# mLSTM chunks of a hybrid decoder layer: all four heads in one step, with q and k loaded a chunk ahead

## The chip, the core and the metric

The kernel runs on one core of a Trainium2 chip. The metric is the device time of one execution in microseconds (us): the median of several runs, where lower is better. The core has five engines that run their own queues of instructions in order: TensorE (PE; its weight loads are listed as PEld), VectorE (DVE), ScalarE (ACT), GpSimd (POOL) and SyncE (SP), which in this kernel issues the DMAs. Matmul results land in PSUM, here in banks of 128x512 f32; everything else on the chip lies in SBUF.

## What is computed

One decoder layer on a 1024 x 1024 input: three token mixers in parallel on the same normalised input (stick-breaking attention, an mLSTM, cross-attention into 256 memory tokens), merged by gates, then a gated MLP with a depthwise convolution. The change concerns the mLSTM alone. It has 4 heads of width 128 and walks over the 1024 positions in 8 chunks of 128, carrying a matrix state from chunk to chunk. Per head and chunk the reference computes:

```
b = cumsum(lfc);  log_d = where(causal, b[t] - b[s] + ic[s], -inf)
s = einsum('td,sd->ts', qc, kc) * exp(log_d - m_t)
w_inter = exp(m_inter - m_t)
num = s @ vc + w_inter * (c_st @ qc)
den = sum(s) + w_inter * (n_st @ qc)
h = num / maximum(abs(den), exp(-m_t))
c_new = decay * c_st + einsum('s,sv,sk->vk', wk, vc, kc)
n_new = decay * n_st + einsum('s,sk->k', wk, kc)
...
h_ml = rmsnorm(h, ml_g_out)          # per head, over its 128 channels
y_ml = sigmoid(ml_o) * h_ml
```

## The kernel before, in words

**Staging.** All large projections are done as three f32r matmuls (`mm3`, L148 to L151: high by high, high by low, low by high) in f32 accuracy. The weight of each product is split into a high and a low part just before it is used: ACT copies the high part (L136), DVE subtracts it for the low part (L137). Pairs of projections go through `seven`, a scheme of seven products; each of its units ("dense" units) is a generator with stages of 24, 36 and 24 matmuls of 128x512. `go(n)` lets the dense list run n stages on.

**The mLSTM.** q and k after their convolution, v, the output gate o and the row factors of all chunks lie in DRAM (`qk_d`, `v_d`, `o_d`, `me_d`). `ml_chunk` (L845) does one chunk for half of the heads, `g` = 0 or 1, in four steps. The loop at L952 takes the chunks from 7 down to 0. Per chunk it runs step 1 of both halves, step 3 of the two halves of the chunk before, one dense stage, step 4 of the chunk before, step 2 of both halves, and another dense stage. In this document a *block* is what PE does between two dense stages in the middle of a chunk: the transposes of step 4 for the chunk before, and then step 2.

- Step 1: load q, k (L848), v (L852) and two sets of row factors, broadcast to 128 partitions (L855); mask the first set on POOL (L858) and take its exponentials on ACT, one per head (L864); scale q by the second set on POOL (L865); k times q on PE (L868) into a bank of the `z` ring, k transposed (L873) into the `tr` ring; DVE multiplies the scores by the exponentials (L869) and scales the transposed k (L876).
- Step 2: numerator and denominator on PE (L883, L884), a bank of `tr`; the new state (L888), a bank of `z`; DVE updates the state (L895) and works out the divisor (L902 to L905); ACT divides while it copies out (L908), squares and sums (L910, one read of the accumulator each); the gate is loaded (L912).
- Step 3: `rstd_cols` (one small DVE operation, L155, and a power on POOL, L157); DVE scales h by it (L916).
- Step 4: transposes on PE (L920) into `tr`; DVE multiplies by g_out and by the gate (L922); store (L923).

**Buffers.** Each of the PSUM rings `tr` and `z` has two banks here. q, k and v of a half share one tile of the `y` ring, which has two buffers: so the two halves of a chunk hold both, and a next chunk's load has to wait until the matmuls of step 2 (L884, L888), which read v, are done. The row factors use the `me` ring (two buffers).

**Order.** The text is written in one order for all engines; a scheduler then sets each engine's queue, so that work from the dense units lies between the steps, and puts in the waits. All DMAs of the stretch stand in SP's one queue.

Of the kernel before, what the change touches and what calls it, by code (L numbers as in the profile page):

```python
# [42 lines left out]
def tile_hybrid_layer(ctx: ExitStack, tc: tile.TileContext, xT, memT, vecs, w_t, w_n, w_kv, w_if,  # L43
# [16 lines left out]
    def nm(s):  # L60
# [4 lines left out]
            "mw": 8, "sm": 22, "px": 2}  # L65
    late = [None]

    def T(shape, tag, dt=F32, bufs=None):
        pool = {"mw": mlp, "mst": mlp, "ga": mlp, "gm": mlp,  "px": late[0]}.get(tag, sb)
        return pool.tile(shape, dt, tag=tag, name=nm(tag), bufs=bufs or BUFS[tag])  # L70
# [444 lines left out]
    def rows_tile():  # L515
        return T([R, P], "mw")

    def suffix(cur, op):
        s = 1
        while s < P:  # L520
            nxt = rows_tile()
# [9 lines left out]
    def gate_rows():  # L531
        gi, gf = rows_tile(), rows_tile()
# [3 lines left out]
        e = rows_tile()  # L536
        nc.scalar.activation(e, gf, AF.Abs)
        nc.scalar.activation(e, e, AF.Exp, scale=-1.0)
        u = rows_tile()
        nc.vector.tensor_scalar(u, e, 1.0, None, op0=ALU.add)  # L540
        lu = rows_tile()
# [5 lines left out]
        bcur = rows_tile()  # L547
        nc.vector.scalar_tensor_tensor(bcur, gf, 0.0, lu, op0=ALU.min, op1=ALU.subtract)

        bcum = suffix(bcur, ALU.add)  # L550
        ga = T([R, P], "ga", bufs=1)
        nc.vector.tensor_sub(ga, gi, bcum)
        amax = suffix(ga, ALU.max)
# [18 lines left out]
        gm = T([R, P], "gm", bufs=1)  # L572
        nc.gpsimd.tensor_scalar(gm, amax, mprev, -1.0, op0=ALU.max, op1=ALU.mult)
        ge = rows_tile()
        nc.scalar.activation(ge, gm, AF.Exp, bias=mprev)
        gw = rows_tile()
        nc.scalar.activation(gw, ga, AF.Exp, bias=gm[:, 0:1])
        gfl = rows_tile()
# [229 lines left out]
    cw = const.tile([P, 40], F32, tag="cw", name="cw")  # L808
# [26 lines left out]
    def ml_o(j):  # L835
        def done(g, c):
            nc.scalar.activation(c, c, AF.Tanh, scale=0.5)
            nc.vector.tensor_scalar(c, c, 1.0, 0.5, op0=ALU.add, op1=ALU.mult)
            nc.sync.dma_start(o_d[j + g], c)
# [3 lines left out]
    def ml_chunk(g, c, state, hm, kw):  # L843
        hd = (2 * g, 2 * g + 1)
        qv = T([P, 4 * P + 258], "y")  # L845
        qk = qv[:, :4 * P].rearrange("p (i h t) -> p i h t", i=2, h=2)
        for i in range(2):
            nc.sync.dma_start(qk[:, i], qk_d[4 * i + 2 * g:4 * i + 2 * g + 2, :, ts(c)].rearrange("h p t -> p h t"))  # L848
        q, k = qk[:, 0], qk[:, 1]
        vx = qv[:, 4 * P:].rearrange("p (h v) -> p h v", h=2)  # L850
        nc.gpsimd.memset(vx[:, :, 128:129], 1.0)
        nc.sync.dma_start(vx[:, :, :P], v_d[c, :, 256 * g:256 * g + 256].rearrange("p (h v) -> p h v", h=2))  # L852
        me = T([P, 2, 2, P], "me")
        for i in range(2):
            nc.sync.dma_start(me[:, i].rearrange("p h t -> p (h t)"),  # L855
                              me_d[i, 4 * c + 2 * g:4 * c + 2 * g + 2].rearrange("h t -> (h t)")
                              .partition_broadcast(P))
        nc.gpsimd.affine_select(out=me[:, 0], in_=me[:, 0], pattern=[[0, 2], [-1, P]], compare_op=ALU.is_ge,  # L858
                                fill=-1e30, base=0, channel_multiplier=1)
        dt_ = T([P, 2, P], "mw")  # L860
        qt = T([P, 2, P], "mw")
        for i, h in enumerate(hd):
            r = 4 * c + h
            nc.scalar.activation(dt_[:, i], me[:, 0, i], AF.Exp, bias=cols[:, 0, r:r + 1])  # L864
            nc.gpsimd.tensor_mul(qt[:, i], q[:, i], me[:, 1, i])  # L865
        pz = bank("z")
        for i in range(2):
            nc.tensor.matmul(pz[:, ts(i)], k[:, i], q[:, i], start=True, stop=True)  # L868
        nc.vector.tensor_mul(dt_.rearrange("p h t -> p (h t)"), dt_.rearrange("p h t -> p (h t)"), pz[:, :2 * P])  # L869
        if c > 0:  # L870
            pk = bank("tr")
            for i, h in enumerate(hd):
                nc.tensor.transpose(pk[:, ts(i)], k[:, i], ident)  # L873
            for i, h in enumerate(hd):
                r = 4 * c + h
                nc.vector.tensor_scalar(kw[:, i], pk[:, ts(i)], cols[:, 1, r:r + 1], None, op0=ALU.mult)  # L876
        yield
        pn = bank("tr")
# [528 lines left out]
```

## Time and profile before

| what | us |
|---|---|
| runs, median (lowest to highest of 3) | 1693.62 (1692.54 to 1694.19) |
| the profiled execution, its own time | 1690.06 |
| its span, first to last instruction | 1688.3 |
| PE busy in the span | 1654.0 (98%) |
| DVE, ACT, POOL busy in the span | 1196.5, 822.9, 72.1 |
| the mLSTM chunks, first to last PE instruction | from 533.7 to 677 in the span |

A span is the time on the profiler's clock from the first to the last instruction; the execution's own time has some 2 us more around it. A wait is an idle stretch of an engine with what ended it. In the timeline, consecutive instructions of one kind are merged into one row ("x4"), and matmuls overlap: what a matmul costs is the distance to the start of the next, not its own duration.

### The profile page before, as it was taken

The page shows a single profiled execution, that of the slowest core. Times are in us where ns is not written, and L with a number is a line of the kernel's source. Part 1 is how long each engine was busy: PE and PEld are TensorE (multiplying, and loading weights), DVE is VectorE, ACT ScalarE, POOL GpSimd, SP SyncE. Part 2 cuts the span into 40 slices and gives each one's busy share as a digit, 9 for nine tenths or more (in the row PEclk, how much of TensorE's full clock was granted, in tenths as well). Part 3 has the DMA queues.
Part 4 walks back from the last instruction along what each step waited for, and adds up shares of the span by engine and source line. Part 5 has one row for each costly group of instructions (what it writes and reads, how often), then busy time and mean ns, then how long its engine had stood idle before and what let it go on. Part 6 is the DMA issues. An engine that isn't in the chain of part 4 may idle for free.

```text
span 1688.3 us, 21433 instructions
## 1 busy us (share of the span) xinstructions
PE 1654.0 (98%) x7927; PEld 1336.0 (79%) x7927; DVE 1196.5 (71%) x1752; ACT 822.9 (49%) x1293; POOL 72.1 (4%) x149
## 2 busy tenths in 40 slices
PE   8999999999999999999999999999999999999999
PEld 4777777787777888777788887788888888788887
DVE  5648777768944665555457748998777887789864
ACT  4547677645545455555412334565545554543531
POOL 1000000020001222100000000000000000000000
PEclk9999999999999999999999999999999999999999
DMA  8421011333325656432765355232322222486042
GB/s 290 150 64 32 26 39 51 106 113 125 122 91 151 168 170 192 145 103 91 253 195 186 107 181 181 69 107 75 103 85 76 75 75 75 162 323 237 30 142 73
DMA packets 99069, 212.73 MB, mean 126 GB/s; under 512 B 13184, under 2 KB 41088, under 8 KB 98964
## 3 DMA queue, kind: packets, MB, share of 16 engines
q1 hardware_dynamic: 98964, 211.35, 37.2%
q8 instruction: 63, 1.03, 0.2%
q14 instruction: 42, 0.34, 0.1%
HBM read 156.71 MB, written 54.61 MB: 125 GB/s over the span
## 4 chain that ended last, share of the span: by engine, by line
PE 83%; DVE 5%; DMA 5%; ACT 4%; issue 1%; SPq 0%; POOL 0%; POOLq 0%; ACTq 0%; DVEq 0%
PE ps_pj L149 13%; PE ps_pj L150 13%; PE ps_pj L151 13%; PE ps_pv L150 5%; PE ps_pv L151 5%; PE ps_pv L149 5%; PE ps_tr L149 4%; PE ps_tr L151 4%; PE ps_tr L150 4%; PE ps_z L151 2%; PE ps_z L150 2%; PE ps_z L149 2%; PE ps_tr L434 1%; PE ps_pv L448 1%; DMA y<-qk_d 1%
## 5 line engine op out<-in xcount | busy, mean ns | idle before, releaser
L150 PE MATMUL ps_pj<-h,whi 128*128 128x512 f32 x620 | 243.4, 393 | 0.0
L136 ACT ACTIVATE whi<-raw 128x512 fp32r<-128x512 f32 (+1 forms) x112 | 93.6, 835 | 184.1 <-PE ps_pj L150 89.0
L149 PE MATMUL ps_pj<-h,whi 128*128 128x512 f32 x412 | 163.6, 397 | 0.5 <-DVE U L1050 0.5
L149 PE MATMUL ps_pj<-pg,whi 128*128 128x512 f32 x396 | 155.2, 392 | 0.9 <-ACT U L708 0.9
L151 PE MATMUL ps_pj<-pg,wlo 128*128 128x512 f32 x380 | 148.1, 390 | 0.2 <-DVE wlo L137 0.2
L150 PEld LDWEIGHTS ps_pj<-h,whi 128*128 128x128 f32 x620 | 116.5, 188 | 24.5 <-issue 1.0
L151 PE MATMUL ps_pj<-h,wlo 128*128 128x512 f32 x332 | 130.8, 394 | 0.5 <-DVE wlo L137 0.4
L818 DVE SCALAR_TENSOR_TENSOR y<-U,vec,y 128x1023 f32<-128x1023 f32 x88 | 112.4, 1279 | 7.7 <-ACT y L816 7.7
L422 DVE TENSOR_TENSOR_SCAN U<-U 128x512 f32<-128x512 f32 (+3 forms) x96 | 88.6, 965 | 30.6 <-ACT U L415 29.7
L149 PEld LDWEIGHTS ps_pj<-h,whi 128*128 128x128 f32 x412 | 77.4, 188 | 17.1 <-DVE U L1050 0.9
L137 DVE TENSOR_TENSOR wlo<-raw,whi 128x1024 fp32r<-128x1024 f32 x54 | 66.0, 1222 | 33.5 <-ACT whi L136 33.5
L149 PEld LDWEIGHTS ps_pj<-pg,whi 128*128 128x128 f32 x396 | 74.3, 188 | 18.1 <-ACT U L708 1.5
L151 PEld LDWEIGHTS ps_pj<-pg,wlo 128*128 128x128 f32 x380 | 71.3, 188 | 15.7 <-DVE wlo L137 0.6
L136 ACT ACTIVATE whi<-pg 128x512 fp32r<-128x512 f32 (+1 forms) x59 | 43.4, 737 | 74.6 <-PE ps_pv L150 20.1
L150 PE MATMUL ps_pj<-pg,whi 128*128 128x512 f32 x188 | 74.8, 398 | 0.0
L151 PEld LDWEIGHTS ps_pj<-h,wlo 128*128 128x128 f32 x332 | 62.3, 188 | 14.7 <-DVE wlo L137 1.4
L150 PE MATMUL ps_pv<-h,whi 128*128 128x512 f32 x164 | 63.8, 389 | 0.0
L137 DVE TENSOR_TENSOR whi<-raw,whi 128x512 fp32r<-128x512 f32 x58 | 40.4, 696 | 31.7 <-ACT whi L136 31.7
L816 ACT ACTIVATE y<-U,vec 128x1024 f32<-128x1024 f32 x44 | 54.6, 1241 | 14.5 <-DVE U L721 14.4
L151 PE MATMUL ps_pj<-h,whi 128*128 128x512 f32 x156 | 60.8, 390 | 0.0
L151 PE MATMUL ps_tr<-pg,wlo 128*128 128x512 f32 x144 | 56.1, 389 | 0.0
L137 DVE TENSOR_TENSOR wlo<-raw,wlo 128x512 fp32r<-128x512 f32 x58 | 40.3, 694 | 21.3 <-ACT wlo L136 21.0
(429 smaller groups left out, 4294.8 us busy)
## 6 DMA issues: line engine op xcount, KB each, us to landing
raw<-in_w_t_dram SPq DMA_DIRECT2D x29, 512.0 KB, 4.9
gate_d<-U SPq DMA_DIRECT2D x24, 512.0 KB, 3.4
U<-gate_d SPq DMA_DIRECT2D x24, 512.0 KB, 3.7
pg<-in_w_up_dram SPq DMA_DIRECT2D x22, 512.0 KB, 3.4
act_d<-y SPq DMA_DIRECT2D x22, 512.0 KB
pg<-in_w_t_dram SPq DMA_DIRECT2D x21, 512.0 KB, 3.3
raw<-in_w_dn_dram SPq DMA_DIRECT2D x18, 512.0 KB, 4.6
raw<-in_w_o_dram SPq DMA_DIRECT2D x16, 512.0 KB, 3.7
```

The lines of the kernel that those rows point to most:

```text
L136: nc.scalar.activation(hi, src, AF.Copy)
L137: (eng or nc.vector).tensor_sub(lo, src, hi.bitcast(F32))
L149: nc.tensor.matmul(out, lh, rh, start=start, stop=False, skip_group_check=more)
L150: nc.tensor.matmul(out, lh, rl, start=False, stop=False, skip_group_check=more)
L151: nc.tensor.matmul(out, ll, rh, start=False, stop=stop, skip_group_check=more)
L422: nc.vector.tensor_tensor_scan(f[:, a, 1:w + 1], f[:, a, 1:w + 1], f[:, a, 1:w + 1], 1.0 if o == 0 else f[:, a, 0:1], op0=ALU.mult, op1=AL ...
L434: nc.tensor.transpose(pt[:, a, ts(j)], g[:, a, ts(j)], ident)
L448: nc.tensor.matmul(pv[64 * a:64 * a + 64, ts(rb % 4)], sbv[s // 2][:, s % 2, (2 * p + a) * 64:(2 * p + a + 1) * 64], wt[:, a, ts(j)], star ...
L816: nc.scalar.activation(out, u, AF.Identity, bias=bias, scale=taps[0])
L818: nc.vector.scalar_tensor_tensor(out[:, :S - s], u[:, s:], taps[s], out[:, :S - s], op0=ALU.mult, op1=ALU.add)
```

## The change

`ml_chunk` handles all four heads of a chunk in one call. Elementwise operations on 128x128 or 128x256 become one on 128x512, with the per-head factors broadcast along the last axis. q and k of a chunk share one `y` tile, and a new function `ml_load` loads them with the row factors of the next chunk right after step 1 of the present one, and before the dense stage. v has two buffers of its own from the `hf` ring for the whole loop (`vx`), with the ones column written once. Scaling q moves from POOL to DVE. The squares are taken by one ACT operation and summed by a DVE reduction. g_out is multiplied into the gate o before that is stored (`ml_o`), so that step 4 multiplies once. A copy of the decay of each head is taken on POOL (`dec`). The buffers of the gate rows are recut so that the `mw` ring needs four buffers of 128x512 and not eight of 128x256. The matmuls are the same in number and shape.

```diff
-    def ml_chunk(g, c, state, hm, kw):
...
+    def ml_load(c):
+        qk = T([P, 2, MLH, P], "y")
         for i in range(2):
-            nc.sync.dma_start(me[:, i].rearrange("p h t -> p (h t)"),
...
+            nc.sync.dma_start(qk[:, i], qk_d[4 * i:4 * i + 4, :, ts(c)].rearrange("h p t -> p h t"))
+        rows = []
         for i in range(2):
+            rows.append(T([P, MLH, P], "me"))
+            nc.sync.dma_start(rows[i].rearrange("p h t -> p (h t)"),
+                              me_d[i, 4 * c:4 * c + 4].rearrange("h t -> (h t)").partition_broadcast(P))
+        return qk[:, 0], qk[:, 1], *rows
+
+    def ml_chunk(c, loaded, state, vx, hm, kw):
...
+        for g in range(2):
+            nc.sync.dma_start(vx[g][:, :, :P], v_d[c, :, 256 * g:256 * g + 256].rearrange("p (h v) -> p h v", h=2))
+        dt_ = T([P, MLH, P], "mw")
+        qt = T([P, MLH, P], "mw")
+        for h in heads:
+            nc.scalar.activation(dt_[:, h], mm[:, h], AF.Exp, bias=cols[:, 0, r0 + h:r0 + h + 1])
+        dec = small(MLH)
+        nc.gpsimd.tensor_copy(dec, ee[:, :, 0])
+        nc.vector.tensor_mul(qt, q, ee)
...
+        nc.vector.tensor_mul(dt_, dt_, pz)
...
+            nc.vector.tensor_mul(kw, pk, spread_cols(cols[:, 1, r0:r0 + 4]))
         yield
...
+        for g in range(2):
+            pn = bank("tr")[:, :258].rearrange("p (h v) -> p h v", h=2)
             for i in range(2):
...
+                nc.tensor.matmul(pn[:, i], dt_[:, h], vx[g][:, i], start=first, stop=True)
+            if c > 0:
+                pst = bank("z")[:, :258].rearrange("p (h v) -> p h v", h=2)
...
+        nc.scalar.activation(qt, hm, AF.Square)
+        ss = small(MLH)
+        nc.vector.tensor_reduce(ss, qt, axis=AX.X, op=ALU.add)
...
+        rr = rstd_cols(ss, MLH, MLD)
+        nc.vector.tensor_mul(hm, hm, spread_cols(rr))
         yield
...
+        nc.vector.tensor_mul(og, py, og)
...
+    loaded = ml_load(NCH - 1)
     for c in range(NCH - 1, -1, -1):
...
+        new = ml_chunk(c, loaded, state, vx, kept[:, 0], kept[:, 1])
+        next(new)
+        if old:
+            next(old)
+        if c:
+            loaded = ml_load(c - 1)
         go(1)
+        if old:
+            next(old)
+        next(new)
         go(1)
```

PE's queue at the block of chunk 6, before (ps_tr and ps_z are banks of the two rings, mst the state, mw the factors, pg h or the scaled k, y holds q, k, v):

```order
L920 MATMUL ps_tr_4651<-ident,pg_4364 128x128 x2
L920 MATMUL ps_tr_4657<-ident,pg_4364 128x128 x2
L888 MATMUL ps_z_4668<-y_4544,pg_4364 128x129 x2
L888 MATMUL ps_z_4689<-y_4570,pg_4364 128x129 x2
...
L883 MATMUL ps_tr_4663<-mst_4459,mw_4556 128x129
L884 MATMUL ps_tr_4663<-y_4544,mw_4555 128x129
```

The same block of the changed kernel (hf are the two tiles of v):

```order
L916 MATMUL ps_tr_4587<-ident,pg_4342 128x128 x4
L883 MATMUL ps_tr_4595<-mst_4430,mw_4512 128x129
L884 MATMUL ps_tr_4595<-hf_4343,mw_4511 128x129
...
L888 MATMUL ps_z_4600<-hf_4343,pg_4342 128x129 x2
L883 MATMUL ps_tr_4610<-mst_4443,mw_4512 128x129
L884 MATMUL ps_tr_4610<-hf_4344,mw_4511 128x129
```

The four transposes now fill one bank, and the second numerator (ps_tr_4610) takes that same bank again within the block, after the first numerator and the first state update.

SP's queue around the loads for chunk 5, before (y are the two tiles of q, k and v of that chunk, raw and pg are weights):

```order
L689 DMA raw_4910<-in_w_t_dram 128x1024
L692 DMA pg_5224<-in_w_t_dram 128x1024
L923 DMA y_d<-mw_4471 128x2x128
...
L848 DMA y_4741<-qk_d 128x2x128 x2
L852 DMA y_4741<-v_d 128x2x128
L855 DMA me_4746<-me_d 128x256 x2
L848 DMA y_4767<-qk_d 128x2x128 x2
```

In the changed kernel the loads of q and k for chunk 4 (y_4697) stand ahead of those of v for chunk 5 (hf):

```order
L680 DMA raw_4798<-in_w_t_dram 128x1024
L838 DMA y_4697<-qk_d 128x4x128 x2
L683 DMA pg_5049<-in_w_t_dram 128x1024
L918 DMA y_d<-mw_4453 128x4x128
L858 DMA hf_4343<-v_d 128x2x128
...
L842 DMA me_4700<-me_d 128x512
```

The q and k loads moved one chunk forward in the queue; the v loads and the row factors did not move as far.

POOL's queue, before, from chunk 5 to chunk 4 (sm in L157 is the power of step 3 of chunk 5, half by half; the mask L858 is on the row factors of chunk 4):

```order
L157 TENSOR_TENSOR sm_5007<-sm_5005,nhalf 128x2
L858 AFFINE_SELECT me_4958<-me_4958 128x256
L157 TENSOR_TENSOR sm_5013<-sm_5011,nhalf 128x2
L865 TENSOR_TENSOR mw_4965<-y_4953,me_4958 128x128 x2
L858 AFFINE_SELECT me_4984<-me_4984 128x256
```

After, from chunk 6 to chunk 4 (the powers sm_4694, sm_4869, sm_5037 are those of chunks 6, 5 and 4; the masks me_4700, me_4875, me_5043 those of chunks 4, 3 and 2):

```order
L157 TENSOR_TENSOR sm_4694<-sm_4692,nhalf 128x4
L855 AFFINE_SELECT me_4700<-me_4700 128x512
L864 COPY sm_4852<-me_4702 128x4
L855 AFFINE_SELECT me_4875<-me_4875 128x512
L157 TENSOR_TENSOR sm_4869<-sm_4867,nhalf 128x4
L864 COPY sm_5020<-me_4877 128x4
L855 AFFINE_SELECT me_5043<-me_5043 128x512
L157 TENSOR_TENSOR sm_5037<-sm_5035,nhalf 128x4
```

The products with q are gone from POOL; the mask of the chunk after next stands ahead of the power for chunks 5 and 4.

DVE's queue, before, from the scaling of h in chunk 4 (sm_5212 and sm_5218 are the two powers) to the products of its block (raw and wlo are a weight page and its low part):

```order
L916 TENSOR_SCALAR pg_4364<-pg_4364,sm_5212 128x128 x2
...
L916 TENSOR_SCALAR pg_4364<-pg_4364,sm_5218 128x128 x2
...
L715 TENSOR_TENSOR raw_5222<-raw_5222 128x512
L137 TENSOR_TENSOR wlo_5319<-raw_4910,wlo_5319 128x512
...
L137 TENSOR_TENSOR whi_5337<-pg_4912,whi_5337 128x512
L703 TENSOR_TENSOR pg_5526<-raw_5524,pg_5526 128x512
L137 TENSOR_TENSOR wlo_5419<-raw_5222,wlo_5419 128x512
L700 TENSOR_TENSOR U_5243<-U_5243,ps_pv_5227 128x512
L922 SCALAR_TENSOR_TENSOR mw_5084<-ps_tr_5265,vec,mw_5084 128x128 x2
L922 SCALAR_TENSOR_TENSOR mw_5105<-ps_tr_5271,vec,mw_5105 128x128 x2
```

After, at the same place:

```order
L912 TENSOR_TENSOR pg_4342<-pg_4342,sm_5037 128x512
L706 TENSOR_TENSOR raw_5047<-raw_5047 128x512
L137 TENSOR_TENSOR wlo_5133<-raw_4798,wlo_5133 128x512
L705 TENSOR_TENSOR U_4973<-U_4973,ps_pv_4975 128x512
L869 TENSOR_TENSOR mw_5014<-mw_5014,ps_z_5023 128x512
L874 TENSOR_TENSOR pg_4342<-ps_tr_5029,cols 128x512
L137 TENSOR_TENSOR whi_5151<-pg_4800,whi_5151 128x512
L694 TENSOR_TENSOR pg_5303<-raw_5301,pg_5303 128x512
L137 TENSOR_TENSOR wlo_5207<-raw_5047,wlo_5207 128x512
L691 TENSOR_TENSOR U_5068<-U_5068,ps_pv_5052 128x512
L917 TENSOR_TENSOR mw_4956<-ps_tr_5090,mw_4956 128x512
```

The order is the same, but for one scaling, one product of the scores, one scaled k and one product with the gate, each 512 wide, in place of two or four smaller ones. The low part that stands third here frees the weight page into which raw_5301 of the eighth row is loaded.

## Rows read from the trace of the kernel before

**Rows 1.** The page: its head and the busy times of the whole span.

```profile
span 1688.3 us, 21433 instructions
...
PE 1654.0 (98%) x7927; PEld 1336.0 (79%) x7927; DVE 1196.5 (71%) x1752; ACT 822.9 (49%) x1293; POOL 72.1 (4%) x149
```

**Rows 2.** Waits, 520 to 690 us (who <- releaser: us in total, times, longest us).

```profile
PE ps_z L868 <- DMA y<-qk_d: 5.8, 4, 2.2
PE ps_pj L149 <- ACT U L708: 1.1, 2, 0.9
...
DVE pg L916 <- POOL sm L157: 22.6, 16, 3.7
```

**Rows 3.** Timeline of PE (start us, us, operation; in brackets idle before, releaser).

```profile
588.83 0.68 PE L868 MATMUL ps_z<-y 128*128 128x128 f32 x4 [1.60 <-DMA y<-qk_d]
...
644.88 0.68 PE L868 MATMUL ps_z<-y 128*128 128x128 f32 x4 [2.20 <-DMA y<-qk_d]
```

**Rows 4.** Timeline of SP, 560 to 605 us: a load of q and k.

```profile
583.07 0.90 SPq L848 DMA_DIRECT2D y<-qk_d  x2
```

**Rows 5.** Landing times of DMAs: q and k, row factors, weights (last column, page).

```profile
DMA to landing us min/median/max: 2.4/3.2/4.6
...
DMA to landing us min/median/max: 3.9/5.6/6.2
...
raw<-in_w_t_dram SPq DMA_DIRECT2D x29, 512.0 KB, 4.9
```

**Rows 6.** Timeline of PE over one chunk: step 1, the block, the next step 1.

```profile
551.66 0.60 PE L868 MATMUL ps_z<-y 128*128 128x128 f32 x4
...
558.49 0.60 PE L920 MATMUL ps_tr<-ident,pg 128*128 128x128 f32 x4
558.92 1.06 PE L888 MATMUL ps_z<-y,pg 128*128 128x129 f32 x8
559.74 0.48 PE L149 MATMUL ps_pj<-h,wlo 128*128 128x512 f32 x1
560.05 0.45 PE L883 MATMUL ps_tr<-mst,mw 128*128 128x129 f32 x2
...
561.82 0.48 PE L150 MATMUL ps_pj<-h,wlo 128*128 128x512 f32 x1
...
567.15 0.60 PE L868 MATMUL ps_z<-y 128*128 128x128 f32 x4
```

**Rows 7.** Timeline of DVE at the same block.

```profile
558.69 0.69 DVE L700 TENSOR_TENSOR U<-U,ps_pv 128x512 f32<-128x512 f32 x1 [0.88 <-PE ps_pv L151]
559.29 1.12 DVE L922 SCALAR_TENSOR_TENSOR mw<-ps_tr,vec,mw 128x128 f32<-128x128 f32 x4
```

**Rows 8.** DVE by shape, 528 to 690 us (count | busy us, mean ns | idle before, releaser).

```profile
L916 DVE TENSOR_SCALAR pg<-pg,sm 128x128 f32<-128x128 f32 x32 | 9.7, 343 | 22.6 <-POOL sm L157 22.6
...
L714 DVE TENSOR_TENSOR U<-U,ps_pv 128x512 f32<-128x512 f32 x7 | 4.8, 684 | 7.9 <-ACT U L713 7.9
```

**Rows 9.** ACT by shape, 528 to 690 us: the squares.

```profile
L910 ACT ACTIVATE mw<-pg 128x128 f32<-128x128 f32 x32 | 9.6, 310 | 0.0
```

**Rows 10.** Timeline of ACT at the same block: the copies out of step 2.

```profile
562.57 0.63 ACT L908 ACTIVATE pg<-ps_tr,sm 128x128 f32<-128x128 f32 x2 [3.25 <-DVE sm L905]
...
563.68 0.61 ACT L908 ACTIVATE pg<-ps_tr,sm 128x128 f32<-128x128 f32 x2
```

**Rows 11.** POOL by shape, 528 to 690 us: the powers and the mask.

```profile
L157 POOL TENSOR_TENSOR sm<-sm,nhalf 128x2 f32<-128x2 f32 x16 | 11.2, 699 | 22.4 <-DVE sm L155 22.4
L858 POOL TENSOR_SCALAR_AFFINE_SELECT me<-me 128x256 f32<-128x256 f32 x14 | 6.0, 432 | 29.6 <-DMA me<-me_d 29.6
L157 POOL TENSOR_TENSOR sm<-sm,nhalf 128x8 f32<-128x8 f32 x1 | 2.0, 2011 | 2.9 <-DVE sm L155 2.9
```

**Rows 12.** Timeline of POOL: a power behind a mask that waits for its rows.

```profile
586.77 0.41 POOL L858 TENSOR_SCALAR_AFFINE_SELECT me<-me 128x256 f32<-128x256 f32 x1 [2.68 <-DMA me<-me_d]
587.14 0.70 POOL L157 TENSOR_TENSOR sm<-sm,nhalf 128x2 f32<-128x2 f32 x1
```

More of the change, by code (lines that the diff above doesn't have):

```diff
@@ new lines, in ml_load, with spread_cols @@
+        rows = []
+        for i in range(2):
+            rows.append(T([P, MLH, P], "me"))
[3 more added lines that the diff above has]
+    def ml_chunk(c, loaded, state, vx, hm, kw):
+        q, k, mm, ee = loaded
+        heads = range(MLH)
+        r0 = 4 * c
+        def spread_cols(x):
+            return x.unsqueeze(2).to_broadcast([P, MLH, P])
+        nc.gpsimd.affine_select(out=mm, in_=mm, pattern=[[0, MLH], [-1, P]], compare_op=ALU.is_ge,
+                                fill=-1e30, base=0, channel_multiplier=1)
+        for g in range(2):
[7 more added lines that the diff above has]
+        nc.vector.tensor_mul(qt, q, ee)
+        pz = bank("z").rearrange("p (h t) -> p h t", h=MLH)
+        for h in heads:
+            nc.tensor.matmul(pz[:, h], k[:, h], q[:, h], start=True, stop=True)
+        nc.vector.tensor_mul(dt_, dt_, pz)
+        if c > 0:
+            pk = bank("tr").rearrange("p (h t) -> p h t", h=MLH)
+            for h in heads:
+                nc.tensor.transpose(pk[:, h], k[:, h], ident)
+            nc.vector.tensor_mul(kw, pk, spread_cols(cols[:, 1, r0:r0 + 4]))
@@ L877, in ml_chunk @@
         yield
[L878 removed]
+        rd = small(MLH)
         first = state[0] is None
[L880 to L891 removed]
+        for g in range(2):
+            pn = bank("tr")[:, :258].rearrange("p (h v) -> p h v", h=2)
+            for i in range(2):
+                h = 2 * g + i
+                if not first:
+                    nc.tensor.matmul(pn[:, i], qt[:, h], state[g][:, i], start=True, stop=False)
+                nc.tensor.matmul(pn[:, i], dt_[:, h], vx[g][:, i], start=first, stop=True)
+            if c > 0:
+                pst = bank("z")[:, :258].rearrange("p (h v) -> p h v", h=2)
+                for i in range(2):
+                    nc.tensor.matmul(pst[:, i], kw[:, 2 * g + i], vx[g][:, i], start=True, stop=True)
@@ L904, in ml_chunk @@
[L904 to L912 removed]
+                    state[g] = T([P, 2, 129], "mst", bufs=2)
@@ new lines, in ml_chunk @@
+                    nc.vector.tensor_copy(state[g], pst)
+                else:
+                    for i in range(2):
+                        nc.vector.scalar_tensor_tensor(state[g][:, i], state[g][:, i], dec[:, 2 * g + i:2 * g + i + 1],
+                                                       pst[:, i], op0=ALU.mult, op1=ALU.add)
+            d = rd[:, 2 * g:2 * g + 2]
+            nc.vector.scalar_tensor_tensor(d, pn[:, :, 128], -1.0, cols[:, 2, r0 + 2 * g:r0 + 2 * g + 2],
+                                           op0=ALU.mult, op1=ALU.max)
@@ L923, in ml_chunk @@
-        nc.sync.dma_start(y_d[1][2 * g:2 * g + 2, :, ts(c)].rearrange("h p t -> p h t"), og)
+        py = bank("tr").rearrange("p (h t) -> p h t", h=MLH)
+        for h in heads:
+            nc.tensor.transpose(py[:, h], hm[:, h], ident)
+        nc.vector.tensor_mul(og, py, og)
+        nc.sync.dma_start(y_d[1][:, :, ts(c)].rearrange("h p t -> p h t"), og)
         yield
```

126 lines of the change are left out of this document (28 added, 98 removed).

## Prediction, made before the changed kernel ran

> **What bounds the kernel now.** First the page's head: PE is busy in 98% of the span, 1654.0 of 1688.3 us, and no other engine in more than 79% (the weight loads, which overlap PE) or 71% (DVE) [rows 1]. So a saving on DVE, ACT or POOL counts only if PE waits for that engine. Second the waits in the mLSTM's stretch, to see for what PE waits there: 5.8 us in four waits of L868, the product of k and q, for the load of q and k, and 1.1 us for the copy of a weight's high part, L708 on ACT [rows 2]. These 6.9 us are all that PE can win in this stretch, 0.4% of the kernel. The large wait of the same view is DVE's own, 22.6 us at L916 for POOL's power, in 16 times [rows 2]. PE waits there for nothing, so that wait is covered today. Third the timelines. The longest waits of L868 end at 588.83 (1.60 us) and 644.88 (2.20 us) [rows 3]. The load for the first was issued at 583.07 [rows 4]; loads of q and k take 3.2 us in the median, up to 4.6, from issue to landing [rows 5]. It was issued late since its tile also holds v, which the matmuls of the chunk before still read. The path of the end here is then: block, buffer of `y`, load, L868.
>
> **The matmuls.** They are as many and as large as before, so PE's busy time stays: 0. The rest is a question of waits.
>
> **q and k a chunk ahead.** The load for chunk c-1 stands behind step 1 of chunk c. It needs the other `y` tile, free since step 1 of chunk c+1, and its user comes a whole chunk later. Two blocks are 8.66 us (block to step 1) and 6.83 us (step 1 to block) apart in the shorter chunks, 15.5 us [rows 6], and the load needs at most 4.6 [rows 5]. A few us of queueing in SP's queue remain covered. All four waits go: -5.8 us [rows 2]. Nothing else is late at L868 itself: it needs only q, k and a `z` bank.
>
> **PE's wait for ACT.** ACT loses the accumulator reads and 32 squares of 310 ns (9.6 us in all [rows 9]) for 8 of 512 elements; it waited more than it worked at this place (3.25 us at 562.57 [rows 10]). The L708 wait stems from a weight page that lands late, and SP's queue ahead of it is recut. Bounds: 0 and -1.1 [rows 2]. I take -0.4, since the queue still holds loads ahead of it.
>
> **DVE.** L916 has 32 operations of 343 ns, 9.7 us [rows 8]; now there are 8 of 512 elements, some 0.69 each by L714 [rows 8], 5.5 us. The scores, the scaled k and the gate's product shrink likewise, while scaling q (8 x 0.69 = 5.5 us) comes from POOL, and a reduction is new. DVE is 71% busy and PE doesn't wait for it: 0 as work. Only the times at which DVE gives back a bank or a factor count; they are the next two terms.
>
> **The bank of the block (new).** All four transposes go to one `tr` bank, and the second numerator needs that bank again within the block. Call the block's start t (558.49 in rows 6). The transposes take 0.43 us (558.49 to 558.92), a numerator group 0.89 (half of 560.05 to 561.82) and half of the state updates 0.41 (half of 558.92 to 559.74) [rows 6]: PE asks at t + 1.73. DVE began the product at 559.29, t + 0.80, behind another operation [rows 7]; one of 512 elements takes 0.68 by L714 [rows 8], and so ends at t + 1.48. That is 0.25 us early: 0. One more operation of 0.6 ahead of it (558.69 to 559.29 [rows 7]) gives 0.35 in each of seven blocks, 2.5 us; a whole product in the way gives 7 x 0.7 = 4.9. A gain is excluded, as PE waits for no bank there today. I take 0, since the rows of this very block are the nearest, and keep 0 to 4.9.
>
> **POOL's queue (new).** The mask of chunk c-2 now stands ahead of the power of chunk c for c = 5, 4 and 2 (and 7, where there is slack). It waits for a load into the buffer that the exponentials of chunk c-1 still read; these lie on ACT among the copies out of the block, at 562.57 to 564.3 in the trace of before [rows 10], so I set them done at t + 4.5. The issue takes 0.45 (half of 0.90 [rows 4]), landing 5.6 (3.9 to 6.2 [rows 5]): t + 10.55. The mask has twice the 256 elements that took 432 ns, 0.86 at most; the power of four columns lies between the 699 ns of two and the 2011 of eight, by proportion 1.14 [rows 11]: t + 12.5. Such a blocking shows once in the trace of before: the mask at 586.77 had waited 2.68 us for its rows, with the power right behind it [rows 12]. What is queued behind the power's user: DVE's scaling of h (0.69, t + 13.2), then up to six operations of some 0.6, then the block's product (0.68), on which PE waits through the bank. For chunk 5, six stand between: t + 17.5; PE asks at t + 15.5 + 1.73 = t + 17.2: 0.3 us. For chunk 2, four stand between: t + 16.3, no wait. For chunk 4, a low part behind the scaling frees a weight page (t + 14.4); its load lands 4.9 later [rows 5], t + 19.3, and a sum, a low part, another sum and the product follow, 0.69 + 0.6 + 0.69 + 0.68: t + 22.0. This chunk has 12 more dense matmuls at 0.23 us (561.82 to 567.15 holds 23 [rows 6]): PE asks at t + 17.2 + 2.8 = t + 20.0, a wait of 2.0. Together +2.3 us. Lower bound 0 (the exponentials come early, the rows land in 3.9); the upper one is a rival.
>
> A wide operation makes its users wait until it is whole: the bank, today freed in quarters, comes free in one piece, which is the wait priced above at 0 by rows 6 and 7. The Trainium skill ("Perfetto Trace Analysis", section "Optimizing Scalar/DVE Operations") speaks against this change: "If Scalar/Vector aren't saturated, but are causing bubbles on other engines, breaking up instructions may allow work to be completed sooner." By that, the wide product would cost PE a bubble at each block; no row here shows such a bubble yet, and the rival that follows from it is the third below.
>
> **Sum.** -5.8 - 0.4 + 0 + 2.3 = -3.9 us. The profiled execution took 1690.06; that gives 1686.2. The median of the runs is 1693.62, 3.6 higher than the profiled execution; the same step from there gives **1689.7 us**. About 0.2% (3.4 us) is what a measurement of this kernel can tell from no change, so this is just beyond it.
>
> **The rivals.**
>
> 1. *Nothing new arises.* The bank is in time, and the rows land before the power is due. For: DVE's present 22.6 us of waiting cost PE nothing. Against: the order of POOL's queue. -5.8 - 0.9 = -6.7: 1686.9.
> 2. *q and k are loaded no earlier in effect.* Their issue stands in SP's one queue behind loads that wait for weight pages, so it comes when it came before. For: all loads of the stretch share that queue. Against: the order has the loads a chunk ahead, and 15 us of slack. 0: 1693.6.
> 3. *The bank of the block decides.* DVE has one more operation ahead of the wide product: 7 x 0.35 = 2.5. For: only 0.25 us of room. Against: rows 7 have the product in time. -3.9 + 2.5 = -1.4: 1692.2.
> 4. *Slower: POOL's queue blocks DVE in three chunks.* Where the row factors land x us after t + 10.55, the scaling, the weight page behind it and the product are x later in each. The waits become 0.3 + x, x - 0.9 and 2.0 + x. At x = 3.5 (for instance the load queued behind a weight load of 4.9 [rows 5]) they are 3.8, 2.6 and 5.5, in all 11.9; less 6.2 it is +5.7: 1699.3. It passes zero at x = 1.6 (1.9 + 0.7 + 3.6 = 6.2) and the 0.2% at x = 2.7. For: the mask waited 29.6 us for rows in this stretch already [rows 11]. Against: two loads a chunk take the place of four.
>
> **How the numbers follow.** The forecast has 0.45: its own range of 1687.4 to 1691.5 lies mostly below the 1690.2 that counts as faster, so 0.36 of it is faster and 0.09 the same. Rival 1 has 0.17, faster. Rival 2 has 0.11 and rival 3 has 0.13, the same; rival 4 has 0.14, 0.11 of it slower. Faster 0.53, same 0.36, slower 0.11. The range goes from 1685.8 (rival 1 and a little of the matmuls' own scatter) to 1695.5, which leaves out most of rival 4 and little else.
>
> **What the changed profile would show.** Right: no wait of L868 for q and k; a PE wait of about 2 us in chunk 4, at the second numerator, released by DVE; a mask on POOL that waits for its rows right ahead of a power in chunks 5 and 4; PE busy 1654 as before. Wrong: waits for the load at the product of k and q (rival 2); a wait of some 0.35 us at the second numerator in every block (rival 3); DVE waiting over 5 us at one scaling of h, and PE behind it at the block (rival 4); PE waits outside of 533 to 690 us that were not there before, which this working takes as unchanged.

## The result, and the profile after

| | kernel before | changed kernel |
|---|---|---|
| median of four runs, us | 1693.90 (1692.54 to 1695.92) | 1683.33 (1682.28 to 1685.04) |
| ratio, with its 95% interval | | 0.9938 (0.9920 to 0.9955) |
| profiled execution, us | 1690.06 | 1682.28 |
| its span, us | 1688.3 | 1680.5 |

The changed kernel is faster by 10.6 us in these runs. A second set (the experiments below) gave 1684.50 against 1692.48, ratio 0.9949 (0.9936 to 0.9962). The forecast of 1689.7, 4 us below the kernel before, had the sign right and less than half of the size, and the time lies below its range (1685.8 to 1695.5).

The head of the page of the changed kernel: PE's busy time is 1.8 us below that of [rows 1], with as many matmuls.

```profile
span 1680.5 us, 21066 instructions
...
PE 1652.2 (98%) x7927; PEld 1337.1 (80%) x7927; DVE 1193.2 (71%) x1682; ACT 819.1 (49%) x1237; POOL 51.8 (3%) x95
```

In its waits from 520 to 690 us there is no row of PE left: the 5.8 and 1.1 us of [rows 2] are gone. What remains is on the other engines (who <- releaser: us in total, times, longest us):

```profile
POOL me L855 <- DMA me<-me_d: 87.8, 6, 37.6
POOL sm L157 <- DVE sm L155: 69.6, 6, 15.2
...
DVE pg L912 <- POOL sm L157: 11.7, 8, 3.3
```

DVE still waits for the power, 11.7 us in place of 22.6, and PE still does not notice.

**How the difference adds up.** From 530 to 700 us both kernels issue the same dense matmuls in the same order, so their starts can be compared one by one, and a wait's cost read as the growth of the distance between two starts. In this stretch the changed kernel gains 9.25 us:

| where | recorded idle before | distance gained |
|---|---|---|
| the four waits of L868 | 5.76 | 6.70 |
| the two waits for L708 (548.80 and 684.62) | 1.09 | 1.63 |
| block in one piece, no dense matmul within it; 0.31 of it at 616.89, a cause that no wait shows | none | 0.80 |
| the rest | none | 0.12 |

Over the whole trace the two profiled spans differ by 7.8 us, as 1.4 us are lost ahead of 530 us. About 1 us of that is a stretch at a lower clock from 417 us on, which the second profile of the kernel before (below) has too.

The first row of the table in two timelines (start, us, operation). Before: step 1 of a chunk, with the wait of 1.60 us of [rows 3] between the second row and the third.

```profile
586.18 0.39 PE L151 MATMUL ps_pv<-h,wlo 128*128 128x512 f32 x1
586.40 0.60 PE L868 MATMUL ps_z<-y 128*128 128x128 f32 x4
...
589.49 0.48 PE L149 MATMUL ps_pj<-h,whi 128*128 128x512 f32 x1
```

After:

```profile
585.13 0.39 PE L151 MATMUL ps_pv<-h,wlo 128*128 128x512 f32 x1
585.36 1.05 PE L868 MATMUL ps_z<-y 128*128 128x128 f32 x8
586.25 0.60 PE L873 MATMUL ps_tr<-ident,y 128*128 128x128 f32 x4
586.61 0.48 PE L149 MATMUL ps_pj<-h,whi 128*128 128x512 f32 x1
```

From the last dense matmul ahead to the first behind, 3.31 us became 1.48: 1.83 (1.84 unrounded) for 1.60 of recorded idle. The wait costs 0.24 more than its idle time, in each of the four places (0.23 to 0.24). Idle time is counted from the modelled end of a matmul (0.39 us behind its start for a dense one), while the next dense matmul usually starts after 0.23 us.

### The profile page after: what moved, and what is told of

The parts are those of the page before. It is cut to its first block, busy times and chain, and to the rows that moved or that the text cites. A ratio compares the mean times of both kernels' runs of the same rounds, so it can differ in the third digit from the quotient of the medians.

```text
span 1680.5 us, 21066 instructions
## 1 busy us (share of the span) xinstructions
PE 1652.2 (98%) x7927; PEld 1337.1 (80%) x7927; DVE 1193.2 (71%) x1682; ACT 819.1 (49%) x1237; POOL 51.8 (3%) x95
## 4 chain that ended last, share of the span: by engine, by line
PE 90%; DVE 4%; ACT 4%; DMA 1%; issue 1%; SPq 0%; POOLq 0%; ACTq 0%; DVEq 0%
PE ps_pj L150 14%; PE ps_pj L149 14%; PE ps_pj L151 14%; PE ps_pv L151 6%; PE ps_pv L149 6%; PE ps_pv L150 6%; PE ps_tr L149 4%; PE ps_tr L151 4%; PE ps_tr L150 4%; PE ps_z L151 2%; PE ps_z L150 2%; PE ps_z L149 2%; PE ps_tr L434 2%; PE ps_pv L448 1%; PE ps_z L226 1%; PE ps_z L1005 1%
## 5 line engine op out<-in xcount | busy, mean ns | idle before, releaser
L436 ACT ACTIVATE y<-ps_tr 128x1024 f32<-128x1024 f32 (+3 forms) x48 | 39.1, 814 | 31.6 <-PE ps_tr L434 31.2
```

Of the source, the lines that this page charges most:

```text
L436: nc.scalar.activation(wt[:, :, :w], pt[:, :, :w], AF.Copy)
```

## The experiments

Each kernel ran on a chip with the kernel before beside it; the ratio is to that one.

**The two kernels once more.** No edit.

> The kernel before once more, unchanged, against itself. Its profiled execution took 1690.06 us, its runs 1692.5 to 1695.9. Theory V (the waits for q and k differ from execution to execution, and the profile caught a mild one): ratio 1.000, and a second profile shows more than 5.8 us of PE waiting for q and k, or waits of the same size elsewhere. Rival F (the two kernels differ elsewhere, all through the span): the second profile's waits for q and k are 5.8 us again within 0.5, and its span is longer by some other rows.

Measured: 1693.98 against 1692.48, ratio 1.0002 (0.9993 to 1.0012). The second profile has 5.1 us of waits for q and k, so theory V's larger wait did not come. Nor do the two kernels differ elsewhere, as rival F had it: the second profiles of both (a2 below is that of the changed kernel) differ by 9.2 us, and 9.7 are gained from 530 to 700 us alone. The span of a1 is 1692.9, 4.6 us longer than the first; by distances some 3.5 us of growth lie behind 700 us. Part of it is in no wait. After the wait of 2.21 us at 644.49, the dense matmuls run 0.43 us apart for eight instructions:

```profile
644.49 0.68 PE L868 MATMUL ps_z<-y 128*128 128x128 f32 x4 [2.21 <-DMA y<-qk_d]
...
645.61 0.63 PE L150 MATMUL ps_pj<-h,whi 128*128 128x512 f32 x1
646.03 0.63 PE L151 MATMUL ps_pj<-h,whi 128*128 128x512 f32 x1
```

By stretches (us, busy times by engine, then the granted clock, DMA share, GB/s), the granted clock in that place was 0.55, mostly the lower level of 1.2 GHz:

```profile
640.00:645.00 5.00, 2.79 (x18) 2.31 (x17) 1.78 (x4) 1.82 (x5) 1.97 (x4) 1.00 0.74 185
645.00:648.00 3.00, 3.00 (x11) 2.44 (x10) 2.56 (x8) 0.69 (x2) 1.28 (x3) 0.55 0.69 231
```

In the first profile the same wait (2.20 us, [rows 3]) was followed by this:

```profile
645.00:648.00 3.00, 3.00 (x17) 2.58 (x18) 1.94 (x5) 0.53 (x2) 0.72 (x2) 1.00 0.84 266
```

So a wait of the same length is paid a second time in one execution (8 x 0.20, 1.6 us) and not in another. Each of the profiles but the first shows at least one such stretch behind a wait, near 417 or near 1065 us or at both; the first profile of before has none (clock 1.000), and only three of the 72 other runs of that kernel were faster. The clock of 68 of these is on record: three have 1.000 and took 1689.78 to 1691.04 us, and the 25 with 0.997 took 1694.6 in the mean. The Trainium skill ("TensorE: Matmul & The Clock Gate", section "What's actually happening") says that the window over which activity is judged is free-running and "doesn't reset when your kernel starts". By that, one and the same wait may or may not lower the clock; the two traces agree with it.

> The changed kernel once more, for a tighter ratio and a second profile. Ratio expected 0.9938 (0.992 to 0.9955 so far), that is 1683 where the kernel before takes 1693.6; no wait of PE for q and k, and PE idle in 533 to 690 us below 0.5 us.

Measured: 1684.50, ratio 0.9949 (0.9936 to 0.9962); no wait of PE for q and k, as expected.

**One half of the change: v apart.** In the kernel before; q and k of the four heads then come in two loads and not in four:

```diff
-        qv = T([P, 4 * P + 258], "y")
+        qk = T([P, 2, MLH, P], "y")
...
+    vx = [T([P, 2, 129], "hf") for _ in range(2)]
```

> The kernel before with one part of the change: q and k of a chunk share a tile, v has two tiles of its own, so that the next chunk's q and k no longer wait for the matmuls that read v. The text order of the loads and all narrow operations stay. Theory B (the buffer is what matters): all of the gain, ratio 0.9935 to 0.996, no PE wait for q and k. Rival W (the wide operations and the emptier POOL bring part of it): some -6 us, ratio 0.9965, and waits for ACT or DVE remain in 533 to 690 us.

Measured: 1687.87, ratio 0.9973 (0.9963 to 0.9984). The waits for q and k are gone, and a new one stands there:

```profile
PE ps_tr L883 <- DVE mw L922: 3.6, 2, 2.2
```

This is the wait for DVE and POOL that the prediction feared for the changed kernel, in two of the chunks that it named (5 and 2), but in the narrow kernel. A chunk has two masks there, and in chunk 5 each stands on POOL ahead of a power (the block that uses the h of this chunk began at 592.10):

```profile
584.54 0.41 POOL L858 TENSOR_SCALAR_AFFINE_SELECT me<-me 128x256 f32<-128x256 f32 x1 [14.19 <-DMA me<-me_d]
584.92 0.70 POOL L157 TENSOR_TENSOR sm<-sm,nhalf 128x2 f32<-128x2 f32 x1
588.09 0.41 POOL L858 TENSOR_SCALAR_AFFINE_SELECT me<-me 128x256 f32<-128x256 f32 x1 [2.47 <-DMA me<-me_d]
588.46 0.71 POOL L157 TENSOR_TENSOR sm<-sm,nhalf 128x2 f32<-128x2 f32 x1
```

The rows for the second half landed 3.5 us after those of the first, the second scaling started at 589.21, and twelve DVE operations later the products of the block ran at 595.45 to 596.57, while PE had asked for the bank at 594.

**The other half: wide, but v in the tile again.** The changed kernel with

```diff
-        qk = T([P, 2, MLH, P], "y")
+        halves = [T([P, 4 * P + 258], "y") for _ in range(2)]
```

and the loads written at the chunk's start.

> The changed kernel with that one part undone: q, k and v of a half share a tile again (two buffers hold one chunk), loaded at the chunk's start; all four heads in one wide operation as in the changed kernel (only the scaling of q goes half by half). Theory B: the waits for q and k come back, 5 to 9 us, ratio 0.999 to 1.001. Rival W: the wide operations keep 2 to 4 us, ratio 0.9975 to 0.999.

Measured: 1683.21, ratio 0.9945 (0.9932 to 0.9959), and no PE wait from 520 to 690 us. Both theories fall: with the buffer shared as before, nothing is late. So the shared buffer alone does not make q and k late. SP's queue at the block of chunk 5 (which starts at 575.47 here) shows why: q and k of the second half are issued at 578.96, 3.5 us after the block's start, and the row factors stand behind them.

```profile
576.83 0.37 SPq L924 DMA_DIRECT2D y_d<-mw  x1
577.44 0.90 SPq L841 DMA_DIRECT2D y<-qk_d  x2
578.44 0.43 SPq L863 DMA_DIRECT2D y<-v_d  x1
578.96 0.93 SPq L841 DMA_DIRECT2D y<-qk_d  x2
579.98 0.42 SPq L863 DMA_DIRECT2D y<-v_d  x1
580.49 0.42 SPq L847 DMA_DIRECT2D me<-me_d  x1
```

In the kernel before, that load was issued at 583.07 [rows 4], 5.4 us after the block's start (577.70). The buffer held the first half's load back to 580.07, 2.4 us after that start (2.0 in a4); then this stood in SP's queue ahead of the second half's:

```profile
581.00 0.46 SPq L848 DMA_DIRECT2D y<-qk_d  x1
581.55 0.44 SPq L852 DMA_DIRECT2D y<-v_d  x1
582.09 0.89 SPq L855 DMA_DIRECT2D me<-me_d  x2
```

Each load holds the queue for some 0.45 us.

**Only the order of the loads.** The kernel before, with q and k of both halves first, then v, then the row factors:

```diff
+        for g in range(2):
+            for i in range(2):
+                nc.sync.dma_start(qk[:, i], ...)
+        for g, (_, vx, _) in enumerate(out):
+            nc.sync.dma_start(vx[:, :, :P], ...)
+        for g, (_, _, me) in enumerate(out):
+            for i in range(2):
+                nc.sync.dma_start(me[:, i].rearrange("p h t -> p (h t)"), ...)
```

> The kernel before with another order of the loads alone: q and k of both halves first, then v of both, then the row factors of both. The tiles, their two buffers and all operations stay. Theory Q (PE waited for the second half's q and k since they stood on SP behind v and the row factors of the first half, some 1.4 us of issues, and behind two stores): the four waits shrink from 5.1-5.8 us to below 2, and the time falls by 3 to 6 us, ratio 0.9965 to 0.998. Rival B (the buffer comes free too late, whatever the order): the waits stay above 4 us, ratio 0.999 to 1.001.

Measured: 1688.70, ratio 0.9974 (0.9964 to 0.9985). The four waits for q and k are gone with no buffer freed, which theory Q had; but the row factors, now last and still four loads, came late. The exponentials wait for them, DVE's product with the scores for the exponentials, and so PE waited for DVE instead:

```profile
PE ps_tr L892 <- DVE mw L931: 1.9, 2, 1.1
PE ps_tr L929 <- DVE pg L885: 0.9, 1, 0.9
```

By distances, 6.7 us are won at L868 and 3.4 lost at two blocks.

**Only the squares.** The kernel before with

```diff
-        for i in range(2):
-            nc.scalar.activation(qt[:, i], hm[:, i], AF.Square, accum_out=ss[:, i:i + 1])
+        nc.scalar.activation(qt, hm, AF.Square)
+        nc.vector.tensor_reduce(ss, qt, axis=AX.X, op=ALU.add)
```

> The kernel before with one part of the change: the squares of a half are taken by one ACT operation of 256 elements and summed by a DVE reduction, in place of two with a read of the accumulator each. Theory A (the PE wait of 0.9 us at 548.8 was for a copy that stood on ACT behind these squares): that wait goes or falls below 0.4 us, the four waits for q and k stay at 5 to 6 us, time -0.5 to -1.6 us, ratio 0.9985 to 1.000. Rival S (it stood there since a weight came late through SP's queue): the wait stays, 0.7 to 1.2 us, ratio 0.9995 to 1.0005.

Measured: 1695.00, ratio 1.0014 (1.0005 to 1.0023). The wait for L708 stays:

```profile
549.63 0.50 PE L149 MATMUL ps_pj<-pg,whi 128*128 128x512 f32 x1 [0.85 <-ACT U L708]
```

Theory A falls. The ratio lies above the ranges of both theories: this edit by itself costs some 2 us in the narrow kernel (PE now waits also for DVE, 1.0 us at L883). What L708 was late for is a weight page. On DVE, before and then with v apart:

```profile
540.96 0.69 DVE L702 TENSOR_TENSOR hf<-pg 128x512 f32<-128x512 f32 x1 [4.10 <-DMA pg<-in_w_t_dram]
```

```profile
539.32 0.69 DVE L702 TENSOR_TENSOR hf<-pg 128x512 f32<-128x512 f32 x1 [1.42 <-DMA pg<-in_w_t_dram]
```

The page came 1.6 us sooner there and PE's wait at 548.80 was gone: behind that page lie, in order, DVE's L721, ACT's tanh (L782), the copies out of step 2, the squares and L708. So far this is what rival S named as the cause. In the changed kernel, though, the page came no sooner (its DVE waited for it until 543.38); there DVE's product on which the tanh waits follows one operation behind the page and not four, and the copy (L699, 548.15) stands ahead of the squares. Several things shorten this chain; which of them is enough was not tried one by one.

**v apart, and wide row factors.** a3, with two loads and one mask a chunk in place of two and one for each half:

```diff
-        me = T([P, 2, 2, P], "me")
-        for i in range(2):
-            nc.sync.dma_start(me[:, i].rearrange("p h t -> p (h t)"), ...)
+        for i in range(2):
+            rows.append(T([P, MLH, P], "me"))
+            nc.sync.dma_start(rows[i].rearrange("p h t -> p (h t)"), ...)
...
```

> The kernel with v apart (a3) and one more part of the change: the row factors of all four heads in one tile for each set, two loads and one mask a chunk in place of four and two, and the copy of the decay. All else stays narrow. Theory M (the 3.6 us that PE waited there for DVE in chunks 5 and 2 came from the second mask, whose rows landed 3 us after those of the first, ahead of the second power): the waits at the first numerator fall below 1.5 us, ratio 0.9945 to 0.9965. Rival N (they come from the narrow operations on DVE themselves): they stay above 3 us, ratio 0.9965 to 0.998.

Measured: 1684.49, ratio 0.9949 (0.9936 to 0.9961), and PE's only wait from 520 to 690 us is 0.3 for L708. Theory M holds: the one mask of chunk 5 still stands between the two powers, but its rows land at 586.08, so the second scaling begins at 587.42, 1.8 us ahead of the same in a3.

```profile
586.08 0.64 POOL L853 TENSOR_SCALAR_AFFINE_SELECT me<-me 128x512 f32<-128x512 f32 x1 [1.77 <-DMA me<-me_d]
586.68 0.71 POOL L157 TENSOR_TENSOR sm<-sm,nhalf 128x2 f32<-128x2 f32 x1
```

**The row factors alone.** The kernel before with that edit and nothing else (q, k and v share a tile, all operations but the mask narrow, loads at the chunk's start).

> The kernel before with one part of the change alone: the row factors of a chunk in two tiles of all four heads, with two loads, one mask and a copy of the decay in place of four loads and two masks; q, k and v of a half still share a tile with two buffers, and all else stays narrow. Theory R (what made q and k late was SP's queue: two row-factor loads of the first half ahead of q and k of the second, 0.9 us of issues, and the loads themselves under way): the waits for q and k fall below 1.5 us, no wait for DVE comes, ratio 0.9945 to 0.9965. Rival U (v apart or all wide operations are needed as well): waits of 3 us or more remain, ratio 0.9970 to 0.9995.

Measured: 1684.15, ratio 0.9939 (0.9926 to 0.9953): all of the gain, as far as the intervals tell (by distances some 8 us of the 9.25 in the stretch). PE's waits in the stretch are one row:

```profile
PE ps_pj L149 <- ACT U L708: 0.2, 1, 0.2
```

SP's queue at the block of chunk 5, which starts at 575.88 here:

```profile
579.15 0.46 SPq L862 DMA_DIRECT2D y<-qk_d  x1
579.71 0.44 SPq L866 DMA_DIRECT2D y<-v_d  x1
580.23 0.93 SPq L862 DMA_DIRECT2D y<-qk_d  x2
...
583.23 0.98 SPq L847 DMA_DIRECT2D me<-me_d  x2
```

q and k of the second half are issued 4.35 us after the block's start (5.4 before), and no row-factor load is under way ahead of them; PE takes them at 585.25, so they land within 5.0 us of the issue, against 5.8 before (583.07 to 588.83). With whole tiles the scheduler itself puts the row factors behind q and k.

**Written a chunk ahead or not.** The changed kernel with

```diff
-    loaded = ml_load(NCH - 1)
     for c in range(NCH - 1, -1, -1):
+        loaded = ml_load(c)
         new = ml_chunk(c, loaded, state, vx, kept[:, 0], kept[:, 1])
...
-        if c:
-            loaded = ml_load(c - 1)
```

> The changed kernel with the loads of q, k and the row factors written at the start of their own chunk, not a chunk ahead; the tiles stay. The scheduler's SP queue has them at nearly the same places as in the changed kernel, since their buffers come free as early. Theory O (the place in the text is nothing, the buffers and the number of loads are all): ratio 0.9935 to 0.9960 like the changed kernel, no PE wait for q and k. Rival T (being written a chunk ahead matters): waits for q and k come back, 3 to 6 us, ratio 0.9975 to 1.000.

Measured: 1683.03, ratio 0.9947 (0.9933 to 0.9961), no PE wait from 520 to 690 us. Theory O holds: where the loads are written is nothing here, as the scheduler's SP queue has them in the same order in both kernels. That it places them by when their buffers come free fits this, but was not tested.

**The price of a late scaling.** The changed kernel with more powers ahead of each power, three and then one (a range of 2 in place of 4):

```diff
-        rr = rstd_cols(ss, MLH, MLD)
...
+        for _ in range(4):
+            nc.gpsimd.tensor_tensor(rr, sc, nhalf[:, :MLH], op=ALU.pow)
```

> The changed kernel with three more powers of 1.0 us on POOL ahead of each power of the mLSTM (their results are written over by the last), so that h is scaled some 3 us later in every chunk. Theory L (the cover of the scaling is small, as the prediction had it: in chunks 5 and 2 the product of the block follows it with some 1.3 us of idle DVE between, in chunk 4 a weight page hangs on it): PE waits at the second numerator of a block for DVE, 3 to 8 us in all, ratio to the changed kernel 1.002 to 1.005, so 0.9965 to 1.000 here. Rival C (DVE's idle time takes it up): no such wait over 0.5 us, ratio 0.9935 to 0.9955 as without it.

Measured: 1699.74, ratio 1.0037 (1.0024 to 1.0050), slower than the kernel before and 15 us slower than the changed one: about twice what theory L had at most. PE waits for DVE at the second numerator of four blocks, as that theory said, and once more at the last transposes, where nothing else is left to do:

```profile
PE ps_tr L883 <- DVE mw L921: 6.5, 4, 2.3
PE ps_tr L920 <- DVE pg L916: 2.9, 1, 2.9
```

By distances the blocks that use the h of chunks 7, 5, 4 and 2 grew by 3.0, 2.6, 2.5 and 1.8 us, and the end by 3.0. That is 12.9 of the 16.0 us by which the stretch grew. Behind the blocks for chunks 7 and 4 the granted clock then fell for a while, which is part of the rest:

```profile
566.00:568.00 2.00, 2.00 (x7) 1.62 (x6) 1.27 (x4) 1.96 (x8) 0.00 (x0) 0.50 0.44 129
```

> The changed kernel with one more power of 1.0 us ahead of each power, in place of three. From the runs with 3.2 us of delay, whose blocks in chunks 7, 5, 4 and 2 lost 3.0, 2.6, 2.5 and 1.8 us and whose end lost 3.0, theory L2 (a fixed cover of 0.2 to 1.4 us in each, all later than that is paid in full) expects 0.8, 0.4, 0.3, 0 and 0.8, so 2 to 3 us over the changed kernel: ratio 0.9955 to 0.9970. Rival: cost in proportion to the delay, a third of 16 us, some 5 us: ratio 0.9975 to 0.9985.

Measured: 1684.62, ratio 0.9956 (0.9943 to 0.9969), which the interval cannot tell from the changed kernel. The trace can: from 530 to 700 us it is 2.8 us longer, in the blocks that use the h of chunks 7, 5 and 2 by 0.4, 0.4 and 0.8, and at the end by 0.9. The sum is as expected, though not its distribution (chunk 2 was to have no cost, chunk 4 0.3, chunk 7 twice as much). So the changed kernel scales h with little to spare for chunks 7, 5, 4 and 2 and at the end; in the blocks for chunks 6, 3 and 1 even three more powers cost nothing. In chunk 5 the scaling came here at 589.13, 12.4 us after the start of the chunk's own block (576.74), 2.0 us later than in the changed kernel, and that cost 0.4:

```profile
589.13 0.69 DVE L916 TENSOR_TENSOR pg<-pg,sm 128x512 f32<-128x512 f32 x1 [2.92 <-POOL sm L915]
```

**What follows.** The kernels fall in two groups. With the row factors in two loads and one mask, and no added powers (the changed kernel, a2, a4, b4, c1, d1), the ratio is 0.9938 to 0.9949; with four loads (a3, b1) and q and k no longer late it is 0.9973 or 0.9974. Beside them the other parts of the change, taken together, move the time by nothing that the intervals show (d1 against the changed kernel); of these the squares, tried alone, cost 2 us (b3). Which property of the wide row factors does it (two issues fewer, the place that the scheduler then gives them, or the larger transfer) was not taken apart further; the SP rows show the first two together. The Trainium skill ("Perfetto Trace Analysis", section "DMA Optimizations") states that "Batching multiple small transfers into larger ones (e.g., 2KB → 4KB or 8KB) can dramatically improve throughput". The landing times agree: 5.1 us for a load of 256 KB in the median of d1, 5.6 for one of 128 KB [rows 5]; whether this or the queue brought the gain, no run here shows.

## Why the prediction was wrong in size

Point by point, by its own terms (us; profile against profile, 530 to 700):

| term | predicted | measured | |
|---|---|---|---|
| q and k | -5.8 | -6.7 | idle time taken as the cost of a wait |
| the wait for L708 | -0.4 | -1.6 | taken as part of the bound; all of it went, and at more than its idle |
| bank of the block | 0 | 0 | right |
| POOL's queue | +2.3 | 0 | row factors, and in chunk 4 a weight page, landed sooner than assumed |
| matmuls | 0 | -0.9 | 0.5 of it: a block with a dense matmul within it costs more; the rest is open |
| sum | -3.9 | -9.25 | |

The forecast of the median was 6.4 us too high. Of that, 3.9 are in the profiled execution (1682.28 where 1686.2 was forecast: 5.35 from the table, less 1.4 lost ahead of 530 us), and 2.5 in the step from there to the median.

**The bank** came out to the hundredth: the product ran at 559.47, 0.81 after the block's start at 558.66, forecast 0.80, and PE reached the second numerator at t + 1.78 without a wait. The rule on breaking up instructions that was weighed there (the Trainium skill, "Perfetto Trace Analysis", section "Optimizing Scalar/DVE Operations"; rival 3) therefore did not bear on this place: the trace shows no such bubble. (In the kernel before, the four products free two banks, two products each, and not one bank in quarters.)

```profile
558.66 0.60 PE L916 MATMUL ps_tr<-ident,pg 128*128 128x128 f32 x4
...
560.44 0.39 PE L883 MATMUL ps_tr<-mst,mw 128*128 128x129 f32 x2
```

```profile
559.47 0.68 DVE L917 TENSOR_TENSOR mw<-ps_tr,mw 128x512 f32<-128x512 f32 x1
```

**POOL's queue** is the step that failed, and the term of the sum that was most off: 2.3 us were put on it, and it cost nothing. The mechanism is there: in chunks 5, 4 and 2 the mask waits and the power stands right behind it, as read from the order. The times along this path were taken too long. In chunk 5 (t = 576.78), on SP, POOL and DVE of the changed kernel:

```profile
581.55 0.81 SPq L842 DMA_DIRECT2D me<-me_d  x2
```

```profile
585.50 0.63 POOL L855 TENSOR_SCALAR_AFFINE_SELECT me<-me 128x512 f32<-128x512 f32 x1 [16.06 <-DMA me<-me_d]
586.11 1.01 POOL L157 TENSOR_TENSOR sm<-sm,nhalf 128x4 f32<-128x4 f32 x1
```

```profile
587.14 0.69 DVE L912 TENSOR_TENSOR pg<-pg,sm 128x512 f32<-128x512 f32 x1 [0.90 <-POOL sm L157]
```

The issue was at t + 4.8, as forecast (4.5 to 4.95), but the mask began 3.95 us later, where the landing alone was taken at 5.6, the median of [rows 5]. Mask and power took 0.63 and 1.01 against 0.86 and 1.14. The scaling began at t + 10.4, forecast t + 12.5. In chunks 4 and 2 the mask began 5.3 and 5.2 us after the issue, and the scaling at t + 11.3 and t + 11.6.

Most of the term, 2.0 us, was chunk 4's, through the weight page behind the scaling. There (t = 592.18) DVE shows this:

```profile
603.44 0.69 DVE L912 TENSOR_TENSOR pg<-pg,sm 128x512 f32<-128x512 f32 x1 [3.28 <-POOL sm L157]
...
608.75 0.69 DVE L694 TENSOR_TENSOR pg<-raw,pg 128x512 f32<-128x512 f32 x1 [1.02 <-DMA raw<-in_w_t_dram]
...
611.11 0.68 DVE L917 TENSOR_TENSOR mw<-ps_tr,mw 128x512 f32<-128x512 f32 x1
```

The load of the page was issued at 605.36, behind the low part, as read from the order. The sum that reads it began 3.4 us later, where 4.9 had been taken: at t + 16.6, forecast t + 19.3. So the block's product ended at t + 19.6, forecast t + 22.0, and PE asked for the bank at t + 19.9, forecast t + 20.0.

What follows the scaling in chunk 5 was priced well: in c2, where it came at t + 12.4, the block lost 0.4 us, and the forecast had 0.3 for t + 12.5. a3 shows the same path cost PE 3.6 us where the rows come by halves. Rival 4, the slower one, was thus a real mechanism. In b2 the three chunks that it priced lost 2.6, 2.5 and 1.8 us; the rest of the 16 us came in chunk 7, to which it gave slack, at the end, and at the lower clock.

**q and k.** That the waits go was right, and of the reason given half was missing: "It was issued late since its tile also holds v, which the matmuls of the chunk before still read." The tile does hold the first half's load back, to 2.4 us after the block's start, and 2.3 in d1. But a4, b1 and d1 keep that tile and have no waits; in the kernel before, SP's queue held the second half's load for another 3.0 us (580.07 to 583.07), in d1 for 2.0. The prediction named that queue, as a cover and as rival 2, and did not count its issues ahead of the late load, though [rows 4] has the 0.45 us of each.

**The matmuls** were put at 0 by their count. In the kernel before a dense matmul lies within each block, and block and neighbours then take up to 0.14 us longer; the busy time fell by 1.8 us (1654.0 to 1652.2) with the same 7927 matmuls.

**From the profile to the median.** The step "the same from there" took 3.6 us between the profiled execution and the median as a constant; for the changed kernel it was 1.05 (1683.33 less 1682.28). The first profile of the kernel before was a lucky execution: PE's clock stayed at 1.000 throughout. In a1 one of the waits for q and k is followed by a stretch at the lower clock; in b3, which has these waits too, none is. Without these waits no profile has such a stretch between 530 and 690 us, but for b2 with its late scalings. Of the 1.4 us that the changed kernel lost ahead of 530 us, part is such a stretch too (417 to 420.5: clock 0.54; in the first profile of before 1.00).

What was right: the sign, the chunks in which the mask stands ahead of the power, no wait of L868, PE's work unchanged but for 1.8 us, and little new outside of the stretch (two waits of PE, 0.5 and 0.4 us, ahead of 530 us). The wait of 2 us in chunk 4 did not come; what did come is nearest to rival 1. That a3 and b1 took about the forecast time (1687.9 and 1688.7) does not bear it out: they are other kernels, in which late row factors cost what the changed kernel does not pay.

## What to carry to other kernels

Where loads share one in-order queue, count the issues ahead of the late one, each at its 0.45 us, before blaming the buffer: the row factors in two broadcast loads a chunk and not four brought as much as the whole change. When a wait is removed, price it by the distance between the starts of the work around it, not by the idle time shown; here 6.7 against 5.8 us, and more in those executions in which a lower clock follows. A wait that is read from the order of the queues needs its landing times at both ends: in chunk 4, a scaling 1.2 us sooner and a weight page that took 3.4 us and not 4.9 decided between 2.0 us and nothing.

## What the runs showed of the hardware that was not expected

A wait of 2.2 us of PE is followed by some 3 us at a granted clock of 0.55 in one execution and at 1.00 in another, 1.6 us of difference for one and the same wait. The first dense matmul behind a wait or a foreign block is followed by the next after 0.31 to 0.34 us, where 0.23 is usual. A row-factor load of 256 KB took no longer to land than one of 128 KB: 5.1 us in the median of d1, 5.6 before [rows 5].
